# Summing Strassen-Winograd weight quarters with adding DMA transfers, and FFN 2 without plain tiles

## The chip, the cores and the metric

One core of one Trainium2 chip runs the whole block in one launch. The metric is the device time of the execution in microseconds (us). The kernel before takes 1122.21 us (median of three runs, 1121.78 to 1122.27). TensorE is the matrix engine (PE in the profile; PEld is its weight load), VectorE is DVE, ScalarE is ACT, GpSimd is POOL, and SyncE (SP) issues most transfers.

## The reference

One encoder layer on 512 tokens with 1024 features, in float32:

```python
x = x + 0.5 * swiglu(rmsnorm(x, norm_ffn1), w_ffn1_gu, w_ffn1_down)
h = rmsnorm(x, norm_mix) @ w_in      # 7 x 1024 columns
# RG-LRU branch (conv, two scans) and 2-D neighbourhood attention, gated and summed to y
x = x + y @ w_out
x = x + 0.5 * swiglu(rmsnorm(x, norm_ffn2), w_ffn2_gu, w_ffn2_down)

def swiglu(h, w_gu, w_down):         # D_FF = 2816
    g, u = split(h @ w_gu, 2)
    return (silu(g) * u) @ w_down
```

The change is in the product with `w_gu` of the two feed-forward networks, FFN 1 and FFN 2 (1024 x 5632 each).

## The kernel before, in words

Activations lie with features on the 128 partitions and tokens along the free axis, as eight tiles (k = 0 to 7) of 128 x 512. A float32 product is made of three matmuls: each operand is split into a rounded high part H and the rest L, and H·H, H·L and L·H are added up in PSUM. Activations are split once; each weight tile of 128 x 1024 is loaded by SP (512 KB), copied to H by ScalarE, and L = raw − H is made by VectorE (`split`, lines 136 to 141). There are three raw weight buffers (`wraw`), four H/L pairs (`wh`, `wl`), and four `pair` tiles of the same size as a raw one.

The hidden tiles of an FFN (22 tiles of 128) are made in two ways. The first `NPLAIN` (4 in FFN 1, 2 in FFN 2) are **plain**: a chunk of 24 matmuls of 512 columns for the gate half, another for the up half (`feat_chunk`, lines 165 to 167). The rest go two at a time, in **units**, by the seven products of the Strassen-Winograd scheme (`strassen`; FFN 1 has 9 units, FFN 2 has 10). A unit's weight block is cut into four quarters of 128 x 1024 (numbered 0 to 3 in the source tensor), the activations into quarters by features and tokens. A product is 24 matmuls of 256 columns (line 291). Seven weight operands are needed: the quarters 0, 2 and 3 themselves, and four sums. Tile `a_` starts as quarter 0 and grows in place: + quarter 1 (form s1), + quarter 3 (form s2), + quarter 2 (for the last product, a22). Tile `b_` is quarter 3 (form s4), then + quarter 1 (form s3). VectorE makes these four adds (line 325), from quarters that stay in their tiles. Each operand is split before the next add changes its tile.

TensorE's order in a unit is a11 (into Z), a12 (into Y), s1, the a22 product of the unit before, s2, s4, s3. In the last unit of an FFN a12 comes after s3, and then its own a22. Between them VectorE and ScalarE add up, multiply by the reciprocal root of the norm, and apply SiLU (`gate`, `put`).

`rstd` makes that reciprocal root: four transposes on TensorE (line 213, or four small matmuls in FFN 1), a reduction and a scaling on VectorE, a square root on ScalarE, a reciprocal on VectorE, four more transposes (line 221), and a copy. In FFN 2 it stands between the first two plain chunks. The activation forms s1 to s4 of FFN 2 (`make_forms`) are made while the last tiles of the product with `w_out` come in.

The order within an engine is not written out: the Tile scheduler takes the program's order as its priority, moves work marked `high_priority` ahead, and places the semaphores. The engines then run their queues in order.

Of the kernel before, what the change touches and what calls it, by code (L numbers as in the profile page):

```python
# [9 lines left out]
F32 = mybir.dt.float32  # L10
F32R = mybir.dt.float32r
AF = mybir.ActivationFunctionType
ALU = mybir.AluOpType
# [3 lines left out]
P = 128  # L17
T = 512
D = 1024
KT = D // P  # L20
DFF = 2816
FT = DFF // P
# [20 lines left out]
NLEAD = 6  # L43


NPLAIN = 4, 2

DTAIL = 3

# [2 lines left out]
AHEAD = 4  # L52
# [32 lines left out]
def block_kernel(ctx: ExitStack, tc, a, out):  # L85
    nc = tc.nc
    const = ctx.enter_context(tc.tile_pool(name="const", bufs=1))
    wpool = ctx.enter_context(tc.tile_pool(name="wpool", bufs=3))
    xpool = ctx.enter_context(tc.tile_pool(name="xpool", bufs=1))
# [11 lines left out]
    def nm(s):  # L101
        uid[0] += 1
        return f"{s}_{uid[0]}"
# [3 lines left out]
    def big_t(dt=F32, shape=(P, T), n="b"):  # L107
        return big.tile(list(shape), dt, tag="big", bufs=NBIG, name=nm(n))
# [13 lines left out]
    xd = dram.tile([KT, P, T], F32, name="xd")  # L122
# [22 lines left out]
    def raw_t():  # L145
        return wpool.tile([P, 1024], F32, tag="wraw", bufs=3, name=nm("wraw"))
# [53 lines left out]

        return xh, xl, ssum, one, square

    def rstd(ssum, lead=False):

        pc = aux_t()
        vx = tiny.tile([P, NCB], F32, tag="vx", name=nm("vx"))
        if lead:
            for j in range(NCB):
                nc.tensor.matmul(pc[:, j : j + 1], ssum[:, j * P : (j + 1) * P], ones[:, 0:1], start=True, stop=True)
            nc.vector.tensor_scalar(vx, pc[:, 0:NCB], 1.0 / D, EPS, ALU.mult, ALU.add)  # L210
        else:
            for j in range(NCB):
                nc.tensor.transpose(pc[:, j * P : (j + 1) * P], ssum[:, j * P : (j + 1) * P], ident)
            nc.vector.reduce_sum(vx, pc.rearrange("p (j f) -> p j f", j=NCB), axis=AX.X)
            nc.vector.tensor_scalar(vx, vx, 1.0 / D, EPS, ALU.mult, ALU.add)
        rcol = tiny.tile([P, NCB], F32, tag="rcol", name=nm("rcol"))
        nc.scalar.activation(rcol, vx, AF.Sqrt)
        nc.vector.reciprocal(rcol, rcol)
        ps = aux_t()
        for j in range(NCB):  # L220
            nc.tensor.transpose(ps[:, j * P : (j + 1) * P], rcol[:, j : j + 1].to_broadcast([P, P]), ident)
        r = xpool.tile([P, T], F32, tag="rstd", name=nm("rstd"))
        nc.scalar.activation(r, ps, AF.Copy)
        return r, rcol, vx

# [46 lines left out]

        return S, raw, cut

    def strassen(src, units, A, r, hs, ahead):

        half = T // 2
        prev = {}
        view = lambda t: t.rearrange("p (m t) -> p m t", m=2)

        def product(ps, w, form, first, last):
            H, L = w
            for m in range(2):
                o = ps[:, m * half : (m + 1) * half]
                for k in range(4):
                    c = slice((m * 4 + k) * P, (m * 4 + k + 1) * P)
                    xh_, xl_ = A[form][k]


                    for w_, x_ in ((H, xh_), (H, xl_), (L, xh_)):  # L290
                        nc.tensor.matmul(o, w_[:, c], x_, start=first and m + k == 0 and w_ is H and x_ is xh_,  # L291
                                         stop=m + k == 4 and w_ is L, skip_group_check=True)

        def operand(raw):
            w = hl_t()
            with tc.high_priority():
                split(raw, *w)
            return w

        def gate(t, tok):  # L300
            rr = r[:, tok].unsqueeze(1).to_broadcast([P, 2, half])
            s_ = big_t(n="s")
            nc.vector.tensor_tensor(view(s_), view(t), rr, ALU.mult)
            nc.scalar.activation(s_, s_, AF.Silu)
            return s_

        def put(u, s_, t, tok):
            for m in range(2):
                c = slice(m * half, (m + 1) * half)
                mark["h"] = nc.vector.tensor_tensor(hs[u * 2 + m][:, tok], s_[:, c], t[:, c], ALU.mult)  # L310

        def last_product(p):
            product(p["Z"], p["w"](), "a22", False, True)
            put(p["u"], gate(p["Z"], slice(half, T)), p["u7"], slice(half, T))

        for u in range(units):
            a_, b_ = raw_t(), raw_t()
            d = pair_t().rearrange("p a b -> p (a b)")
            c = pair_t().rearrange("p a b -> p (a b)")

            for t, i in ((a_, 0), (d, 1), (b_, 3), (c, 2)):
                nc.sync.dma_start(t, src[u, i])

            def add(t, o, i):
                nc.vector.tensor_tensor(t, t, o, ALU.add)  # L325
            def after_sum(t, o, i, add=add):
                with tc.high_priority():
                    add(t, o, i)
                return operand(t)

            Z, X, Y = acc_t(), acc_t(), aux_t()
            hs += [big_t(n="h") for _ in range(2)]
            last = u == units - 1

            def gate1():
                product(Y, w_c, "a12", True, True)
                nc.vector.tensor_tensor(p1, p1, Y, ALU.add)
                return gate(p1, slice(0, half))

            product(Z, operand(a_), "a11", True, False)  # L340
            p1 = big_t(n="p1")
            nc.scalar.activation(p1, Z, AF.Copy)
            w_c = operand(c)
            if not last:
                s1 = gate1()
            product(X, after_sum(a_, d, 1), "s1", True, False)
            p5 = big_t(n="p5")
            nc.scalar.activation(p5, X, AF.Copy)
            if prev:
                last_product(prev)  # L350
            product(Z, after_sum(a_, b_, 3), "s2", False, False)
            u2 = big_t(n="u2")
            nc.scalar.activation(u2, Z, AF.Copy)
            product(X, operand(b_), "s4", False, True)
            nc.vector.tensor_tensor(u2, u2, X, ALU.add)
            product(Z, after_sum(b_, d, 1), "s3", False, False)
            nc.vector.tensor_tensor(p5, p5, Z, ALU.add)
            if last:
                ahead()
                s1 = gate1()  # L360
            put(len(hs) // 2 - 1, s1, u2, slice(0, half))
            prev = dict(u=len(hs) // 2 - 1, Z=Z, u7=p5, w=lambda a_=a_, c=c, f=after_sum: f(a_, c, 2))
        last_product(prev)

    def ffn(wgu, ws, wd, xh, xl, S, ssum, plain, res, emit_out, lead=None, end=None):
        hs = []
        r = None
        pre = {}
        if lead is not None:
# [5 lines left out]
            for k in range(KT):  # L375
                lead[0](k)
                if k in LEAD_W:
                    n = LEAD_W[k]
                    o = (k % 4) * P
# [53 lines left out]
        A = {"a11": quarter(0, slice(0, half)), "a12": quarter(4, slice(0, half)),  # L433
             "a22": quarter(4, slice(half, T)), **S}
# [5 lines left out]
        def ahead(n):  # L440
            while len(cuts) < min(n, len(order)):
                qk = order[len(cuts)]
                cuts[qk] = big_t(F32R, n="hh"), big_t(F32R, n="hl")
                split(hs[qk[1]], *cuts[qk])

        strassen(ws, (FT - plain) // 2, A, r, hs, lambda: ahead(AHEAD))
        for q in range(2):
            outs = range(q * 4, q * 4 + 4)
            for i in range(2):
                t = pair_t()  # L450
# [23 lines left out]
            for i, m in enumerate(outs):  # L474
# [4 lines left out]
                t = big_t(n="dn")  # L479
# [50 lines left out]
    xh, xl, ssum, one, square = make_xg(C_G1, "a")  # L530
# [32 lines left out]
    forms = Forms(C_G1)  # L563
# [20 lines left out]
    xh, xl, ssum = nxt["v"][:3]  # L584
# [424 lines left out]
    def out2(m, ps):  # L1009
# [1 line left out]
        nc.vector.tensor_tensor(o, ps, xres[m], ALU.add)  # L1011
        nc.sync.dma_start(out[m], o)

    ffn(a["w2gu"], a["w2s"], a["w2d"], xh, xl, forms.S, ssum, NPLAIN[1], lambda m: xd[m], out2,
        end=lambda tok, o: nc.sync.dma_start(out[KT - 1][:, tok], o[:, tok]))


def layouts(inp):
# [3 lines left out]
    o = {}  # L1022
# [7 lines left out]
    for i in (1, 2):  # L1030
        w = f(f"w_ffn{i}_gu")[0]
        g, u = feat(w[:, :DFF]), feat(w[:, DFF:])
        n = NPLAIN[i - 1]
        o[f"w{i}gu"] = con(np.stack([g, u], 1)[:n]).reshape(2 * n, P, D)

        b = np.stack([g, u], 0)[:, n:].reshape(2, (FT - n) // 2, 2, P, 2, D // 2)
        o[f"w{i}s"] = con(b.transpose(1, 4, 0, 3, 2, 5)).reshape((FT - n) // 2, 4, P, D)
        d = f(f"w_ffn{i}_down")[0].reshape(FT // 2, 2, P, 2, T)
        o[f"w{i}d"] = con(d.transpose(3, 0, 2, 1, 4)).reshape(2, FT // 2, P, 2 * T)
# [50 lines left out]
```

## Time and profile before

| | |
|---|---|
| median of three runs | 1122.21 us |
| profiled execution | 1122.16 us |
| its span, first to last instruction | 1119.9 us |
| TensorE busy | 1113.1 us |
| VectorE busy | 835.1 us |
| ScalarE busy | 593.0 us |
| GpSimd busy | 52.4 us |
| mean DMA rate | 123 GB/s |
| TensorE clock granted | 1.00 |

FFN 1's units run from about 45 to 233 us of the span, the mixing part follows, the product with `w_out` ends at about 772, FFN 2's plain chunks at 795, its units at 997. A row of the page's groups gives line, engine, operation, output and inputs, shapes and count, then busy us and mean ns of one, then the idle time before. A row of the timeline or of the chain begins with start and duration in us. A row of the windows view gives the stretch, its length, then for PE, PEld, DVE, ACT and POOL the busy time and count, then the granted clock, the DMA engines' busy share and GB/s. A DMA row gives count, KB each and the median us from issue to landing.

### The profile page before, as it was taken

How to read it: one execution, taken by the hardware profiler on the slowest of the kernel's cores; microseconds unless marked ns; L12 is line 12 of the kernel's file. 1: busy time of each engine (PE TensorE's matmuls, PEld its weight loads, DVE VectorE, ACT ScalarE, POOL GpSimd, SP SyncE). 2: the span in 40 equal slices, each digit the busy share in tenths (PEclk: the TensorE clock that was granted, in tenths of full speed). 3: DMA queues.
4: the chain of work that ended last, by engine and by line, in shares of the span. 5: the costliest groups of instructions: out<-in, count | busy, mean ns of one | idle time of the engine just before them, and what ended most of it. 6: DMA issues, size and time to landing. Idle time of an engine off the chain costs nothing.

```text
span 1119.9 us, 17423 instructions
## 1 busy us (share of the span) xinstructions
PE 1113.1 (99%) x6867; PEld 983.9 (88%) x6867; DVE 835.1 (75%) x1294; ACT 593.0 (53%) x897; POOL 52.4 (5%) x116
## 2 busy tenths in 40 slices
PE   9999999999999999999999999999999999999998
PEld 8899999988888778787888888888999999998887
DVE  7888888894745776998655976659788888894552
ACT  8554554563533669876464564446445455464330
POOL 0000000000000341310110000000000000000000
PEclk9999999999999999999999999999999999999999
DMA  7232333343433585653443332264134233353421
GB/s 265 95 124 85 113 114 95 120 144 95 136 91 107 160 255 154 184 164 95 144 140 104 104 104 72 75 237 164 57 96 131 77 115 113 94 170 95 132 76 38
DMA packets 46770, 138.04 MB, mean 123 GB/s; under 512 B 7008, under 2 KB 10592, under 8 KB 46688
## 3 DMA queue, kind: packets, MB, share of 16 engines
q1 hardware_dynamic: 39744, 118.31, 33.9%
q0 software_dynamic: 6368, 18.36, 5.8%
q8 instruction: 54, 0.88, 0.3%
q10 hardware_dynamic: 576, 0.26, 0.1%
q14 instruction: 28, 0.23, 0.1%
HBM read 120.12 MB, written 8.39 MB: 115 GB/s over the span
## 4 chain that ended last, share of the span: by engine, by line
PE 99%; DVE 0%; ACT 0%; issue 0%; ACTq 0%; DVEq 0%
PE acc L291 29%; PE acc L165 11%; PE acc L166 11%; PE acc L167 11%; PE aux L291 5%; PE acc L763 4%; PE acc L765 4%; PE acc L764 4%; PE aux L165 4%; PE aux L166 4%; PE aux L167 4%; PE aux L898 1%; PE aux L886 1%; PE aux L677 1%; PE aux L857 1%; PE acc L404 1%
## 5 line engine op out<-in xcount | busy, mean ns | idle before, releaser
L138 ACT ACTIVATE wh<-wraw 128x1024 fp32r<-128x1024 f32 (+3 forms) x242 | 239.7, 993 | 304.3 <-PE acc L291 95.9
L141 DVE TENSOR_TENSOR wl<-wraw,wh 128x1024 fp32r<-128x1024 f32 (+3 forms) x254 | 289.1, 1143 | 135.7 <-ACT wh L138 134.7
L291 PE MATMUL acc<-s,wh 128*128 128x256 f32 x1216 | 220.5, 283 | 0.0
L291 PEld LDWEIGHTS acc<-s,wh 128*128 128x128 f32 x1216 | 189.7, 192 | 0.0
L291 PE MATMUL acc<-s,wl 128*128 128x256 f32 x608 | 172.1, 283 | 0.0
L165 PE MATMUL acc<-xh,wh 128*128 128x512 f32 x304 | 121.1, 399 | 0.0
L167 PE MATMUL acc<-xh,wl 128*128 128x512 f32 x304 | 119.0, 391 | 0.0
L166 PE MATMUL acc<-xl,wh 128*128 128x512 f32 x304 | 118.9, 391 | 0.0
L291 PEld LDWEIGHTS acc<-s,wl 128*128 128x128 f32 x608 | 116.7, 192 | 0.0
L291 PE MATMUL acc<-xh,wl 128*128 128x256 f32 x304 | 86.0, 283 | 0.0
L291 PE MATMUL acc<-xl,wh 128*128 128x256 f32 x304 | 86.0, 283 | 0.0
L291 PE MATMUL acc<-xh,wh 128*128 128x256 f32 x304 | 86.0, 283 | 0.0
L763 PE MATMUL acc<-wh,xh 128*128 128x512 f32 x192 | 75.6, 394 | 0.0
L765 PE MATMUL acc<-wl,xh 128*128 128x512 f32 x192 | 74.9, 390 | 0.0
L764 PE MATMUL acc<-wh,xl 128*128 128x512 f32 x192 | 74.9, 390 | 0.0
L325 DVE TENSOR_TENSOR wraw<-wraw,pair 128x1024 f32<-128x1024 f32 x57 | 69.6, 1220 | 0.8
L165 PE MATMUL aux<-hh,wh 128*128 128x512 f32 (+1 forms) x181 | 69.9, 386 | 0.0
L166 PE MATMUL aux<-hl,wh 128*128 128x512 f32 (+1 forms) x181 | 69.9, 386 | 0.0
L167 PE MATMUL aux<-hh,wl 128*128 128x512 f32 (+1 forms) x181 | 69.9, 386 | 0.0
L165 PEld LDWEIGHTS acc<-xh,wh 128*128 128x128 f32 x304 | 57.1, 188 | 12.8 <-issue 1.7
L167 PE MATMUL acc<-hh,wl 128*128 128x512 f32 (+1 forms) x176 | 67.9, 386 | 0.0
L166 PE MATMUL acc<-hl,wh 128*128 128x512 f32 (+1 forms) x176 | 67.9, 386 | 0.0
(212 smaller groups left out, 2215.6 us busy)
## 6 DMA issues: line engine op xcount, KB each, us to landing
wraw<-wqkv SPq DMA_DIRECT2D x24, 512.0 KB, 4.8
wraw<-wg SPq DMA_DIRECT2D x24, 512.0 KB, 3.6
wraw<-w1d SPq DMA_DIRECT2D x22, 512.0 KB, 3.6
wraw<-w2d SPq DMA_DIRECT2D x22, 512.0 KB, 3.6
pair<-w2s SPq DMA_DIRECT2D x20, 512.0 KB, 3.6
wraw<-w2s SPq DMA_DIRECT2D x20, 512.0 KB, 3.7
wraw<-w1s SPq DMA_DIRECT2D x18, 512.0 KB, 3.6
pair<-w1s SPq DMA_DIRECT2D x18, 512.0 KB, 3.6
```

The lines of the kernel that those rows point to most:

```text
L138: nc.scalar.activation(H, raw, AF.Copy)
L141: nc.vector.tensor_tensor(L, raw, H.bitcast(F32), ALU.subtract)
L165: nc.tensor.matmul(ps, wh, xh, start=first, stop=False, skip_group_check=skip)
L166: nc.tensor.matmul(ps, wh, xl, start=False, stop=False, skip_group_check=skip)
L167: mark["mm"] = nc.tensor.matmul(ps, wl, xh, start=False, stop=last, skip_group_check=skip)
L291: nc.tensor.matmul(o, w_[:, c], x_, start=first and m + k == 0 and w_ is H and x_ is xh_, stop=m + k == 4 and w_ is L, skip_group_check=True)
L325: nc.vector.tensor_tensor(t, t, o, ALU.add)
L404: nc.tensor.matmul(pre[i], w[i][1][:, s], xh[k], start=k == 0, stop=False)
L677: prev, mm = mm, nc.tensor.matmul(ps[d][b], W[w][o, c], X[x][o], start=x == 1, stop=w + x == 0)
L763: nc.tensor.matmul(pss[j], xh[kk][:, tj], H[:, s], start=kk == 0, stop=False)
L764: nc.tensor.matmul(pss[j], xl[kk][:, tj], H[:, s], start=False, stop=False)
L765: mark["mm"] = nc.tensor.matmul(pss[j], xh[kk][:, tj], L[:, s], start=False, stop=kk == KT - 1)
```

## The change

`NPLAIN` becomes 4, 0: FFN 2 has no plain tile and eleven units. In every unit of both FFNs the four adds leave VectorE. A transfer issued by GpSimd reads the quarter from memory and adds it into the tile (`accum_op=ALU.add`): quarters 1, 3 and 2 into `a_`, and quarter 3 into `d`, which was loaded as quarter 1 (form s3; before, it was made in `b_`). A unit so has four loads and four adding transfers of 512 KB each, where it had four loads. In FFN 2 the first products (a11) of units 0 and 1 are made first of all, by `begin`, and `rstd` is called after unit 0's a12, writing into a tile made beforehand.

```diff
-NPLAIN = 4, 2
+NPLAIN = 4, 0
...
+        def begin(u):
+            a_ = raw_t()
+            nc.sync.dma_start(a_, src[u, 0])
+            Z = acc_t()
             product(Z, operand(a_), "a11", True, False)
             p1 = big_t(n="p1")
             nc.scalar.activation(p1, Z, AF.Copy)
+            return a_, Z, p1
+
+        def add(u, t, i):
+            with tc.high_priority():
+                nc.gpsimd.dma_start(t, src[u, i], accum_op=ALU.add)
+
+        begun = {u: begin(u) for u in range(2)} if late is not None else {}
+        for u in range(units):
+            a_, Z, p1 = begun.pop(u) if u in begun else begin(u)
+            b_ = raw_t()
...
-            for t, i in ((a_, 0), (d, 1), (b_, 3), (c, 2)):
+            add(u, a_, 1)
+            for t, i in ((c, 2), (d, 1), (b_, 3)):
                 nc.sync.dma_start(t, src[u, i])
-            def add(t, o, i):
-                nc.vector.tensor_tensor(t, t, o, ALU.add)
+            add(u, d, 3)
...
                 product(Y, w_c, "a12", True, True)
+                if u == 0 and late is not None:
+                    late()
...
-            product(X, after_sum(a_, d, 1), "s1", True, False)
+            w = operand(a_)
+            add(u, a_, 3)
+            product(X, w, "s1", True, False)
...
-            product(Z, after_sum(a_, b_, 3), "s2", False, False)
+            w = operand(a_)
+            add(u, a_, 2)
+            product(Z, w, "s2", False, False)
...
-            product(Z, after_sum(b_, d, 1), "s3", False, False)
+            product(Z, operand(d), "s3", False, False)
...
-            prev = dict(..., w=lambda a_=a_, c=c, f=after_sum: f(a_, c, 2))
+            prev = dict(..., w=lambda a_=a_: operand(a_))
...
+        if r is None:
+            r = xpool.tile([P, T], F32, tag="rstd", name=nm("rstd"))
+            late = lambda: rstd(ssum, False, r)
```

GpSimd's queue of the new kernel, at the start of FFN 2 (`wraw_1429` and `wraw_1434` are the tiles a of units 0 and 1, `pair_1440`, `pair_1464` and `pair_1492` the tiles d of units 0, 1 and 2):

```order
L329 DMA pair_1440_7848<-w2s 128x1024
L329 DMA wraw_1429_7781<-w2s 128x1024
L329 DMA wraw_1434_7814<-w2s 128x1024
L329 DMA pair_1464_8031<-w2s 128x1024
L329 DMA wraw_1429_7781<-w2s 128x1024 x2
L329 DMA pair_1492_8263<-w2s 128x1024
L329 DMA wraw_1434_7814<-w2s 128x1024 x2
```

Before, GpSimd has nothing in this place. The add into the next unit's d now stands between a's first add and its second; the third follows the second.

VectorE's queue of the new kernel at the start of FFN 2, after the first two form splits (`wl_1457`, `wl_1460`, `wl_1462` are L of s2, s4 and s3 of unit 0, `wl_1471` is L of a12 of unit 1, `vx` and `rcol` belong to `rstd`):

```order
L141 TENSOR_TENSOR s2_1423_7769<-s2_1411_7713,s2_1422_7768 128x512
L141 TENSOR_TENSOR s4_1425_7773<-s4_1412_7715,s4_1424_7772 128x512
L141 TENSOR_TENSOR wl_1457_7940<-wraw_1429_7781,wh_1456_7939 128x1024
L141 TENSOR_TENSOR wl_1460_7971<-wraw_1439_7847,wh_1459_7970 128x1024
L141 TENSOR_TENSOR s3_1427_7777<-s3_1413_7717,s3_1426_7776 128x512
L141 TENSOR_TENSOR wl_1462_8000<-pair_1440_7848,wh_1461_7999 128x1024
L214 TENSOR_REDUCE vx_1449_7888<-aux_1448_7887 128x4
L350 TENSOR_TENSOR p1_1433_7812<-p1_1433_7812,aux_1443_7856 128x512
L215 TENSOR_SCALAR vx_1449_7888<-vx_1449_7888 128x4
L141 TENSOR_TENSOR wl_1471_8043<-pair_1465_8032,wh_1470_8042 128x1024
L218 RECIPROCAL rcol_1450_7895<-rcol_1450_7895 128x4
```

Before, the reduction (line 214) stood right behind the first of these rows, and the reciprocal five rows later. Now three weight splits and a form split stand ahead of the reduction, and one more split ahead of the reciprocal.

TensorE's queue of the new kernel at the second transposes of `rstd` (line 221), with the end of s2 of unit 0 ahead (`wh_1456`, `wl_1457`) and a12 of unit 1 behind (`wh_1470`):

```order
L292 MATMUL acc_1430_7783<-s2_1422_7768,wh_1456_7939 128x256
L292 MATMUL acc_1430_7783<-s2_1423_7769,wh_1456_7939 128x256
L221 MATMUL aux_1451_7898<-ident_83,rcol_1450_7895 128x128 x4
L292 MATMUL acc_1430_7783<-s2_1422_7768,wl_1457_7940 128x256
L292 MATMUL aux_1467_8039<-xh_1352_7421,wh_1470_8042 128x256
```

Before, these transposes stood in the second plain chunk. They now stand one matmul before the end of the fifth product of FFN 2.

More of the change, by code (lines that the diff above doesn't have):

```diff
@@ L201, in make_xg, with rstd @@
         return xh, xl, ssum, one, square
-    def rstd(ssum, lead=False):
+    def rstd(ssum, lead=False, r=None):
         pc = aux_t()
@@ L221, in rstd @@
             nc.tensor.transpose(ps[:, j * P : (j + 1) * P], rcol[:, j : j + 1].to_broadcast([P, P]), ident)
-        r = xpool.tile([P, T], F32, tag="rstd", name=nm("rstd"))
+        if r is None:
+            r = xpool.tile([P, T], F32, tag="rstd", name=nm("rstd"))
         nc.scalar.activation(r, ps, AF.Copy)
@@ L273, in make_forms, with strassen @@
         return S, raw, cut
-    def strassen(src, units, A, r, hs, ahead):
+    def strassen(src, units, A, r, hs, ahead, late=None):
         half = T // 2
@@ L314, in last_product @@
             put(p["u"], gate(p["Z"], slice(half, T)), p["u7"], slice(half, T))
+        def begin(u):
+            a_ = raw_t()
+            nc.sync.dma_start(a_, src[u, 0])
+            Z = acc_t()
+            product(Z, operand(a_), "a11", True, False)
+            p1 = big_t(n="p1")
+            nc.scalar.activation(p1, Z, AF.Copy)
+            return a_, Z, p1
[3 more added lines that the diff above has]
+        begun = {u: begin(u) for u in range(2)} if late is not None else {}
         for u in range(units):
-            a_, b_ = raw_t(), raw_t()
+            a_, Z, p1 = begun.pop(u) if u in begun else begin(u)
+            b_ = raw_t()
             d = pair_t().rearrange("p a b -> p (a b)")
             c = pair_t().rearrange("p a b -> p (a b)")
-            for t, i in ((a_, 0), (d, 1), (b_, 3), (c, 2)):
+            add(u, a_, 1)
+            for t, i in ((c, 2), (d, 1), (b_, 3)):
                 nc.sync.dma_start(t, src[u, i])
-            def add(t, o, i):
[L325 to L331, printed above, removed]
+            add(u, d, 3)
+            X, Y = acc_t(), aux_t()
             hs += [big_t(n="h") for _ in range(2)]
@@ L336, in gate1 @@
                 product(Y, w_c, "a12", True, True)
+                if u == 0 and late is not None:
+                    late()
                 nc.vector.tensor_tensor(p1, p1, Y, ALU.add)
                 return gate(p1, slice(0, half))
-            product(Z, operand(a_), "a11", True, False)
-            p1 = big_t(n="p1")
-            nc.scalar.activation(p1, Z, AF.Copy)
             w_c = operand(c)
@@ L361, in strassen @@
             put(len(hs) // 2 - 1, s1, u2, slice(0, half))
-            prev = dict(u=len(hs) // 2 - 1, Z=Z, u7=p5, w=lambda a_=a_, c=c, f=after_sum: f(a_, c, 2))
+            prev = dict(u=len(hs) // 2 - 1, Z=Z, u7=p5, w=lambda a_=a_: operand(a_))
         last_product(prev)
@@ L444, in ahead @@
                 split(hs[qk[1]], *cuts[qk])
-        strassen(ws, (FT - plain) // 2, A, r, hs, lambda: ahead(AHEAD))
+        if r is None:
+            r = xpool.tile([P, T], F32, tag="rstd", name=nm("rstd"))
+            late = lambda: rstd(ssum, False, r)
+        else:
+            late = None
+        strassen(ws, (FT - plain) // 2, A, r, hs, lambda: ahead(AHEAD), late)
         for q in range(2):
@@ L1012, in out2 @@
         nc.sync.dma_start(out[m], o)
-    ffn(a["w2gu"], a["w2s"], a["w2d"], xh, xl, forms.S, ssum, NPLAIN[1], lambda m: xd[m], out2,
+    ffn(None, a["w2s"], a["w2d"], xh, xl, forms.S, ssum, NPLAIN[1], lambda m: xd[m], out2,
         end=lambda tok, o: nc.sync.dma_start(out[KT - 1][:, tok], o[:, tok]))
@@ L1033, in layouts @@
         n = NPLAIN[i - 1]
-        o[f"w{i}gu"] = con(np.stack([g, u], 1)[:n]).reshape(2 * n, P, D)
+        if n:
+            o[f"w{i}gu"] = con(np.stack([g, u], 1)[:n]).reshape(2 * n, P, D)
         b = np.stack([g, u], 0)[:, n:].reshape(2, (FT - n) // 2, 2, P, 2, D // 2)
```

## The prediction

> **What bounds the kernel now.** I read the page first: engines, then the chain that ended last.
>
> ```profile
> span 1119.9 us, 17423 instructions
> ...
> PE 1113.1 (99%) x6867; PEld 983.9 (88%) x6867; DVE 835.1 (75%) x1294; ACT 593.0 (53%) x897; POOL 52.4 (5%) x116
> ...
> PE 99%; DVE 0%; ACT 0%; issue 0%; ACTq 0%; DVEq 0%
> ```
>
> TensorE is busy for 1113.1 of 1119.9 us, and the chain is TensorE all the way. Only two things can shorten the kernel: less TensorE work, or some of its 6.8 idle us. VectorE time as such buys nothing. Where TensorE stands in the two places that the change touches is read from the chain in order of time, FFN 1's start first, then FFN 2:
>
> ```profile
> 56.51 5.65 PE acc L291 x47
> ...
> 62.41 0.95 ACT wh L138
> ...
> 63.41 0.50 PE aux L291 x2
> ```
> ```profile
> 777.68 0.44 PE aux L213 x4
> ...
> 784.72 0.44 PE aux L221 x4
> ...
> 794.93 2.87 PE acc L291 x24
> ...
> 858.29 17.28 PE acc L291 x144
> 875.57 2.88 PE aux L291 x24
> 878.45 17.28 PE acc L291 x144
> 895.73 2.88 PE aux L291 x24
> ```
>
> FFN 1 has one hole, about 0.9 us at 62.4, where a weight operand was late. FFN 2's seven-product units run without one: a product of 24 matmuls takes 2.88 us, a unit 7 x 2.88 = 20.16 us. The windows view shows the four plain chunks and one unit:
>
> ```profile
> 772.24:794.93 22.69, 22.69 (x106) 18.79 (x106) 16.48 (x26) 12.81 (x18) 0.00 (x0) 1.00 0.18 63
> 878.45:898.61 20.16, 20.16 (x170) 20.16 (x170) 17.27 (x21) 10.15 (x13) 0.00 (x0) 1.00 0.34 105
> ```
>
> **The change, part by part. Plain chunks for a unit.** The first window holds the 96 plain matmuls and the 8 transposes of the reciprocal root (2 x 0.44 us): 22.69 - 0.88 = 21.8 us for 96. They go, the transposes stay, and an eleventh unit of 20.16 us comes: -1.6 us. That is the whole of the arithmetic gain, although an eighth of the multiplications is saved, because a 512-column matmul costs 0.227 us and a 256-column one 0.120.
>
> **Adds taken from VectorE.** The groups view has them on one line:
>
> ```profile
> L325 DVE TENSOR_TENSOR wraw<-wraw,pair 128x1024 f32<-128x1024 f32 x57 | 69.6, 1220 | 0.8
> ...
> L325 DVE TENSOR_TENSOR wraw<-wraw,wraw 128x1024 f32<-128x1024 f32 x19 | 23.2, 1220 | 0.1
> ```
>
> 92.8 us leave VectorE. All but FFN 1's hole lies under TensorE, so I credit -0.9 us: in the new order the first unit's fourth and fifth products follow its third, and no add stands before their splits. The transposes of FFN 1's own root move some matmuls earlier there; I put that at nothing, +-0.4 us, as vector work and matmuls stand close on both sides.
>
> **The price of an adding transfer, X** (issue to landing). No row shows one. The nearest rows:
>
> ```profile
> wraw<-w2s SPq DMA_DIRECT2D x20, 512.0 KB, 3.7
> ...
> bm<-rpb POOLq DMA_DIRECT2D x16, 384.0 KB, 4.7
> ...
> wraw<-wgate SPq DMA_DIRECT2D x8, 128.0 KB, 2.8
> ```
> ```profile
> L805 POOL DMA_DIRECT2D bm<-rpb x16: 548/548/608, 405.4 to 649.5; - x16
> ...
> DMA to landing us min/median/max: 3.2/4.7/8.3
> ```
>
> Lower bound: 3.7 us, a plain load of these bytes (the 3.2 us of GpSimd's quickest 384 KB say that its queue alone is no slower). Upper bound: 7.4 us, two such loads one behind the other. In between, 128 to 512 KB cost 0.9 us, so 512 KB of data cost 1.2 us and the rest is fixed; if the transfer must read the old sum as well as the quarter, 3.7 + 1.2 = 4.9. Some traffic beside it adds, up to the 8.3 - 4.7 of the row above at worst; I take X = 5.3 us.
>
> The Trainium skill (Collectives: The Full Stack, "The bandwidth ceiling") says that an adding transfer is slower because it needs two source reads, not because of the addition, with half the rate measured. No run here shows it yet. With the fit of DMA: Bandwidth & Descriptors ("Anatomy of one DMA"), 2.0 us plus bytes over 436 GB/s, that is an estimate of 2.0 + 2 x 1.2 = 4.4 us, and the sum below would be about 1.7 us lower by it.
>
> **What waits for X.** Each split is a ScalarE copy (H) and a VectorE subtraction (L). Of a unit's four adds three hit one tile, a: split, add, split, add, split, add, split. An in-place add may start only when L of the form before has been read out. The timeline of before gives the clock of such splits; they start when a product frees one of four operand buffers:
>
> ```profile
> 884.17 1.06 ACT L138 ACTIVATE wh<-wraw 128x1024 fp32r<-128x1024 f32 x1 [0.44 <-PE acc L291]
> ```
> ```profile
> 885.51 1.21 DVE L141 TENSOR_TENSOR wl<-wraw,wh 128x1024 fp32r<-128x1024 f32 x1
> ...
> 891.14 1.22 DVE L141 TENSOR_TENSOR wl<-wraw,wh 128x1024 fp32r<-128x1024 f32 x1
> ```
>
> For the unit whose a11 product starts at 892.85 (2.88 before 895.73), the first split of a ends at 886.72. The first add then lands at 886.8 + X; H 1.06, L 1.22 and two hand-overs make 2.35, so the second form is split at 889.15 + X, or at 892.36 as before, if that is later. The second add lands at 889.2 + 2X. Its form, s2, is the fifth product, at 892.85 + 4 x 2.88 = 904.37, and needs L by its third matmul, 904.6; less 2.35 that is 902.25. So 2X must stay under 13.05: **a middle unit is covered up to X = 6.5 us.** In GpSimd's queue the next unit's add into d stands behind the first add, but its load landed by then, so it is not waited for. The third add has five products of time.
>
> In each FFN's last unit the a12 product is put behind the others, so s2 comes 2.88 us sooner: covered up to 2X = 10.17, and short by 2X - 10.2 beyond. At 5.3: 0.4 us, twice, +0.8.
>
> **FFN 2's start.** The root now stands behind the first three products. Until 778.6 the order on ScalarE and VectorE is that of before, four plain splits replaced by a11, a11 of the second unit, c and s1, so its times hold:
>
> ```profile
> 773.55 1.22 DVE L141 TENSOR_TENSOR wl<-wraw,wh 128x1024 fp32r<-128x1024 f32 x1
> ...
> 778.62 0.68 DVE L214 TENSOR_REDUCE vx<-aux 128x4 f32<-128x512 f32 x1
> ...
> 782.09 0.68 DVE L141 TENSOR_TENSOR s<-s,s 128x512 fp32r<-128x512 f32 x1
> 782.69 0.16 DVE L215 TENSOR_SCALAR vx<-vx 128x4 f32<-128x4 f32 x1
> 783.12 0.18 DVE L218 RECIPROCAL rcol<-rcol 128x4 f32<-128x4 f32 x1 [0.27 <-ACT rcol L217]
> ```
>
> The fourth split (s1) ends at 774.8; then a's second add goes out, with d's add of the second unit just ahead in the same queue (+0.5), and lands at 774.8 + 5.3 + 0.5 = 780.6. VectorE now has, in order: L of s2, L of s4, the last form's split, L of s3, the reduction, p1 + Y, the scaling, L of the second unit's a12, the reciprocal. H of s2 first, 1.1; then 1.22 + 1.22 + 0.68 + 1.22 + 0.68 + 0.68 + 0.16 + 1.22 + 0.18 = 7.3, less 0.4, as back-to-back instructions overlap by some 0.08 us: the reciprocal is there at 780.6 + 8.0 = 788.6. TensorE reaches the second transposes, one matmul before the end of s2, at 772.24 + 3 x 2.88 + 0.44 + 2.88 + 23 x 0.12 = 786.96, and stands: **+1.6 us**. Behind it stand that matmul, the second unit's a12 and s4; they have their operands by then. s2 itself needs H by 784.2 and has it at 781.7. The stall is X + 0.5 - 4.2; below X = 3.7 it is nothing.
>
> **The sum**, against the profiled execution: 1122.16 us (span 1119.9 and 2.3 around it, 0.05 under the median 1122.21). -1.6 - 0.9 + 1.6 + 0.8 = -0.1, so **1122.1 us**. A measurement here tells 0.2% (2.2 us) from no change.
>
> **The rivals.**
>
> *Faster: the add is nearly free.* X near 3.7: no stall at the start, none in the last units, -2.5 us, 1119.7. For it: the 3.2 us row. Against it: a transfer that reads twice as much would have to take no longer. All gains lie in FFN 1's hole and the 1.6 us, so there is nothing below about 1119.5.
>
> *Slower, by the start and the last units.* X of 5.8 to 6.5, say 6.2: start 2.5, last units 2 x 2.2, so -2.5 + 6.9 = +4.4, 1126.6. For it: the 4.7 us median of GpSimd's loads, with 1.2 for the second read.
>
> *Slower, by the chain of adds in every unit.* One mechanism, split-add-split-add before s2, deciding from X = 6.5: a unit then takes X - 6.5 more (each stall before s2 also starts the next unit's chain that much sooner in its cycle, so 2(X - 6.5) shares out over two). At 7.3: 17 middle units x 0.8 = 13.6, last units 2 x 3.6, start 3.6, less 2.5: +22, 1144. For it: the chain hangs on a latency that nothing here has measured. Against it: the upper bound has to be nearly right.
>
> *Slower, by full DMA engines.* A unit's four loads take 0.34 of 20.16 us, 1.7 each. Four adds at twice that would make 6.9 + 13.7 = 20.6 us, more than a unit: 20 x 0.4, about +9, 1131. The Trainium skill (DMA: Bandwidth & Descriptors, "Issuing engines are not separate DMA queues") is on its side: all transfers share 16 engines, and GpSimd's queue saves only issue time. Against it a stage of before:
>
> ```profile
> 0.00:45.00 45.00, 43.94 (x196) 36.88 (x197) 35.83 (x78) 31.96 (x58) 0.83 (x10) 1.00 0.66 223
> ```
>
> 223 GB/s at a share of 0.66 is 338 at full; the unit would read 6.3 MB in 20.16 us, 312 GB/s. Tight, but under it.
>
> That the change might not do what it says I give nothing: the new order holds 80 adding transfers, and no plain chunk in FFN 2.
>
> **How the numbers follow.** No change 0.47 (X about 3.9 to 5.75, 1120 to 1124.4); faster 0.20; slower by start and ends 0.13; by the chain 0.16; by full engines 0.04. Faster by over 0.2%: 0.20, though its case ends close to that bound; within: 0.47; slower: 0.33. The range is 1119.4, with all holes closed, to 1129, X = 6.5 with start 2.8 and last units 2 x 2.8 (1128) and a little of the chain; most of the chain case is left out.
>
> **What would show it.** The adding transfers' landing time is X; below 3.9, or above 5.8, my case falls. A hole of 1 to 2 us before the second transposes of FFN 2, some 14 us after its first product; none at FFN 1's start; under a microsecond each before s2 of the two last units; units of 20.16 us between. A unit longer than 20.16 would prove the chain, if TensorE waits before s2 for ScalarE's split and that for a transfer; full engines, if the DMA share in the unit is over 0.95. A DMA share of about 0.9 in a unit would bear out the second read, and one near 0.68 would refute it.

## The result, and the profile after

The changed kernel takes **1194.76 us** (median of four, 1191.06 to 1196.26), against 1122.24 for the kernel before: a ratio of 1.0642, 95% interval 1.0629 to 1.0655. The forecast was 1122.1 us, no change, with a range up to 1129.0; the measured time is 72.7 us above it.

The page of the changed kernel: span, busy times, and the adding transfers, whose issue-to-landing time stands at the end of their row.

```profile
span 1193.3 us, 17696 instructions
...
PE 1138.8 (95%) x6939; PEld 1000.4 (84%) x6939; DVE 753.1 (63%) x1226; ACT 587.8 (49%) x903; POOL 120.9 (10%) x196
...
wraw<-w2s POOLq DMA_DIRECT2D x33, 512.0 KB, 5.7
```

VectorE is relieved by 82 us net (the adds alone were 92.8). TensorE now stands idle for 54.5 us where it was 6.8. It is also busy for 25.7 us longer, though its matmuls were to take 1.6 us less: behind some holes its granted clock is halved (the last experiment), and the mean of the matmuls with s and wh on line 292 is 294 ns where the same ones took 283. What it waits for is told by the waits view (engine, tile and line waited for, us in total, times, longest):

```profile
PE acc L292 <- DVE wl L141: 14.6, 20, 0.8
PE acc L292 <- ACT wh L138: 12.9, 15, 2.1
PE acc L292 <- ACT u L367: 10.1, 14, 5.2
PE acc L292 <- ACT p L360: 6.3, 12, 0.5
PE acc L292 <- ACT p L324: 4.6, 1, 4.6
```

Apart from the last row, and from the one of 5.2 us in the third, these are small holes, repeated from unit to unit. One step back, ScalarE's waits show where they come from:

```profile
ACT wh L138 <- DMA wraw<-w2s: 120.8, 21, 7.4
ACT wh L138 <- DMA wraw<-w1s: 106.3, 18, 8.8
```

Before, ScalarE's splits in the units waited for TensorE to free an operand buffer (107.6 us in 87 waits). Now they wait for the transfers into `wraw`, 227 us in 39 waits, about two a unit.

Half of the loss is in each FFN. A wait in the middle of the mixing part, whose order is the same in both kernels, gives the border; first before, then after:

```profile
517.31 0.39 PE L857 MATMUL aux<-kl,qh 64*128 64x256 f32 x2 [0.90 <-DVE kl L840]
```
```profile
551.94 0.39 PE L876 MATMUL aux<-kl,qh 64*128 64x256 f32 x2 [0.91 <-DVE kl L859]
```

So 34.6 us are lost in FFN 1 and 73.4 - 34.6 = 38.8 in FFN 2 with its new start.

**The rhythm of a unit.** ScalarE's timeline shows one unit of FFN 2 from its s1 split to that of the next; GpSimd's gives the adds.

```profile
903.25 2.01 ACT L138 ACTIVATE wh<-wraw 128x1024 fp32r<-128x1024 f32 x2 [6.61 <-DMA wraw<-w2s]
...
911.21 2.00 ACT L138 ACTIVATE wh<-wraw 128x1024 fp32r<-128x1024 f32 x2 [5.46 <-DMA wraw<-w2s]
914.88 0.63 ACT L305 ACTIVATE s<-s 128x512 f32<-128x512 f32 x1 [1.67 <-DVE s L304]
915.42 1.04 ACT L138 ACTIVATE wh<-pair 128x1024 fp32r<-128x1024 f32 x1
916.37 0.58 ACT L360 ACTIVATE p<-acc 128x512 f32<-128x512 f32 x1
916.84 1.05 ACT L138 ACTIVATE wh<-wraw 128x1024 fp32r<-128x1024 f32 x1
...
926.21 2.00 ACT L138 ACTIVATE wh<-wraw 128x1024 fp32r<-128x1024 f32 x2 [5.79 <-DMA wraw<-w2s]
```
```profile
905.93 0.85 POOL L329 DMA_DIRECT2D wraw<-w2s  x1 [6.21 <-DVE h L311]
913.88 0.87 POOL L329 DMA_DIRECT2D wraw<-w2s  x1 [7.10 <-DVE wl L141]
919.94 0.87 POOL L329 DMA_DIRECT2D wraw<-w2s  x1 [5.19 <-DVE wl L141]
```

Each pair "x2" is two splits: at 903.25 s1 and the a22 of the unit before, at 911.21 s2 and s4. The s1 split starts at 903.25 and is read out by 905.6. The second add goes out at 905.93 and has landed by 911.21, where s2 is split. Behind s2 on ScalarE stand s4, a SiLU, s3 (`pair`) and the copy of the s1 product; only at 916.84 comes the split of the **next unit's a11**. When VectorE has read that out, the next unit's first add may start, at 919.94; it lands, and the next s1 split starts at 926.21. (The add at 913.88 is the third, for a22.) This is a closed loop: 2.7 + 5.3 + 5.6 + 3.1 + 6.3 = 23.0 us, of which 5.3 and 6.3 are landings and 11.4 splits and queues. TensorE's 20.16 us of work are not in it.

From 72.19 to 235.73 there are seven such rounds in FFN 1, 23.36 us each; from 855.66 to 1041.97 eight in FFN 2, 23.29 each:

```profile
72.19 2.01 ACT L138 ACTIVATE wh<-wraw 128x1024 fp32r<-128x1024 f32 x2 [8.76 <-DMA wraw<-w1s]
...
235.73 2.01 ACT L138 ACTIVATE wh<-wraw 128x1024 fp32r<-128x1024 f32 x2 [5.20 <-DMA wraw<-w1s]
...
855.66 2.01 ACT L138 ACTIVATE wh<-wraw 128x1024 fp32r<-128x1024 f32 x2 [7.40 <-DMA wraw<-w2s]
...
1041.97 2.01 ACT L138 ACTIVATE wh<-wraw 128x1024 fp32r<-128x1024 f32 x2 [5.24 <-DMA wraw<-w2s]
```

These 15 rounds lose 7 x 3.20 + 8 x 3.13 = 47 us of the 73. The other 26 lie in the first and last units and are only in part itemised here, by two single holes: 4.62 us before FFN 2's fifth product, and 5.16 us in FFN 1's last unit, where s3 waits for ScalarE's copy of the s2 product, which stands behind the split of a22, and that behind the third add, which landed after 8.8 us.

```profile
823.40 0.80 PE L292 MATMUL acc<-s,wh 128*128 128x256 f32 x2 [4.62 <-ACT p L324]
```
```profile
257.14 0.80 PE L292 MATMUL acc<-s,wh 128*128 128x256 f32 x2 [5.16 <-ACT u L367]
```

### The profile page after: what moved, and what is told of

Same layout as the page of the kernel before. It is cut to its first block, busy times and chain, and to the rows that moved or that the text cites. A ratio compares the mean times of both kernels' runs of the same rounds, so it can differ in the third digit from the quotient of the medians.

```text
span 1193.3 us, 17696 instructions
## 1 busy us (share of the span) xinstructions
PE 1138.8 (95%) x6939; PEld 1000.4 (84%) x6939; DVE 753.1 (63%) x1226; ACT 587.8 (49%) x903; POOL 120.9 (10%) x196
## 5 line engine op out<-in xcount | busy, mean ns | idle before, releaser
L141 DVE TENSOR_TENSOR wl<-wraw,wh 128x1024 fp32r<-128x1024 f32 (+3 forms) x236 | 267.0, 1137 | 293.4 <-ACT wh L138 287.6
L138 ACT ACTIVATE wh<-wraw 128x1024 fp32r<-128x1024 f32 (+3 forms) x224 | 216.4, 983 | 398.5 <-DMA wraw<-w2s 120.8
L292 PE MATMUL acc<-s,wh 128*128 128x256 f32 x1280 | 248.8, 294 | 34.0 <-ACT wh L138 12.9
L292 PEld LDWEIGHTS acc<-s,wh 128*128 128x128 f32 x1280 | 207.7, 200 | 43.0 <-ACT wh L138 16.3
L292 PE MATMUL acc<-s,wl 128*128 128x256 f32 x640 | 188.4, 294 | 14.6 <-DVE wl L141 14.6
L292 PEld LDWEIGHTS acc<-s,wl 128*128 128x128 f32 x640 | 127.7, 200 | 18.9 <-DVE wl L141 18.7
L165 PE MATMUL acc<-xh,wh 128*128 128x512 f32 x272 | 108.6, 399 | 0.0
L167 PE MATMUL acc<-xh,wl 128*128 128x512 f32 x272 | 106.4, 391 | 0.0
L166 PE MATMUL acc<-xl,wh 128*128 128x512 f32 x272 | 106.3, 391 | 0.0
L165 PE MATMUL acc<-hh,wh 128*128 128x512 f32 (+1 forms) x176 | 67.9, 386 | 0.0
```

Source lines behind the costliest of these rows:

```text
L138: nc.scalar.activation(H, raw, AF.Copy)
L141: nc.vector.tensor_tensor(L, raw, H.bitcast(F32), ALU.subtract)
L165: nc.tensor.matmul(ps, wh, xh, start=first, stop=False, skip_group_check=skip)
L166: nc.tensor.matmul(ps, wh, xl, start=False, stop=False, skip_group_check=skip)
L167: mark["mm"] = nc.tensor.matmul(ps, wl, xh, start=False, stop=last, skip_group_check=skip)
```

## The experiments

**Theories.** A: the loop just read off sets a unit's time. B: the transfer engines are too full (busy 0.78 in the units), so that bytes set it. C: FFN 2's new start is what costs. D, tried last: TensorE's halved clock after the holes.

**The price of one adding transfer.** Edit, behind the last output of the kernel before:

```diff
+    t = raw_t()
+    for kind in ("sync", "pool", "add"):
+        for n in (1024, 512, 256):
+            for j in range(3):
+                q = nc.sync if kind == "sync" else nc.gpsimd
+                kw = dict(accum_op=ALU.add) if kind == "add" else {}
+                i = q.dma_start(t[:, :n], w[j, 0][:, :n], **kw)
+                after(i, prev, True)
+                prev = i
```

> The kernel before, with 27 transfers put behind its last output, each waiting for the one ahead: plain loads issued by SyncE, plain loads issued by GpSimd, adding transfers issued by GpSimd, three each of 512, 256 and 128 KB, into one idle tile. Nothing else moves then. Theory A (the adding transfer is dear by itself): 512 KB by adding takes at least 5.0 us from issue to landing, against 3.7 for a plain load, and falls by over 1 us at 256 KB. Theory B (it is dear in the units because the transfer engines are crowded there): under 4.5 us alone, and the 5.7 us of the changed kernel is mostly queueing. The time of this kernel is that of before plus the probes and says nothing.

The landing times (least, median, most of three), for 512 KB loaded plainly by GpSimd, and then for 512, 256 and 128 KB by adding, each from its own stretch:

```profile
DMA to landing us min/median/max: 3.8/3.9/4.0
```
```profile
DMA to landing us min/median/max: 5.7/5.7/5.8
```
```profile
DMA to landing us min/median/max: 3.5/3.8/3.8
```
```profile
DMA to landing us min/median/max: 3.0/3.0/3.1
```

With nothing beside it an adding transfer of 512 KB takes **5.7 us**, as the median in the units does. That price is its own, not queueing; B's reason for the 5.7 falls. Single landings in the changed kernel go from 5.2 to 12.7 us, so neighbours do add to it at times.

**The adds without the new start.** FFN 2 keeps two plain tiles; the rest is as changed.

```diff
-NPLAIN = 4, 0
+NPLAIN = 4, 2
```

> The adding transfers alone: FFN 2 keeps its two plain tiles, its root between them, and 10 units. Theory A (a closed loop of two adds and the splits between them, 23 us a round, in every unit of both FFNs): FFN 1 as in the changed kernel, +34 us, and FFN 2's 10 units +2.7 us each with its last unit, so 1180 to 1190 us. Theory C (the loss of FFN 2 comes from its new start, two first products and the late root): 1122 + 34 = 1156 to 1162 us.

Measured 1191.15 us in a single run, 3.6 less than the changed kernel's median and inside the spread of its four runs. Nearly all of the loss is there without the new start, whose own price cannot be read from this run; C falls as the main cause, and A's 1180 to 1190 was just missed.

**The new start without the adding transfers.**

```diff
-            add(u, a_, 1)
-            add(u, d, 3)
...
-            w = operand(a_)
-            add(u, a_, 3)
-            product(X, w, "s1", True, False)
+            product(X, after_sum(a_, d), "s1", True, False)
...
```

(with the three other sums in the same way by VectorE)

> The eleven units and the late root alone: FFN 2 without plain tiles, its first two products ahead, the four sums of every unit made by VectorE as before. Theory A: no loop over transfers, units of 20.16 us; four plain chunks for a unit, -1.6 us, and at most 1 us lost at FFN 2's start, so 1120 to 1122 us. Theory C (the new start loses): 1125 us or more, with a hole ahead of the fifth product or of the root's second transposes.

Measured 1126.09 us, ratio 1.0038 (1.0025 to 1.0050): 0.4% slower than before, where A had 1120 to 1122. One hole explains most of it:

```profile
786.08 0.39 PE L292 MATMUL acc<-s,wh 128*128 128x256 f32 x1 [4.23 <-DVE s L141]
```

The s1 product waits for the last split of its activation form; C had put the hole later, ahead of the fifth product or the second transposes. Four sums by VectorE now stand between the parts of the forms, where before four plain chunks gave 21.8 us of cover. Behind the hole the granted clock is 0.85 and 0.72 (784 to 788, 788 to 792), an estimated 1.7 us. So C is real in this kernel, at some 4 us and what the clock adds; and the two halves of the change need each other, since with the adds on transfers this hole is not there.

**The next unit's first product sooner.**

```diff
             nc.scalar.activation(u2, Z, AF.Copy)
+            if u + 1 < units and u + 1 not in begun:
+                begun[u + 1] = begin(u + 1)
```

> The changed kernel with one edit: the first product of the next unit is made right behind s2 of this one, two products sooner, so that its split stands ahead of those of s4 and s3 on ScalarE and VectorE, and the next add into its tile does not wait for them. The transfers and their bytes are the same. Theory A (closed loop, 2 landings + 11.4 us of splits and queues between): the 11.4 fall to about 7.5, the loop to 19 us, under the 20.16 us of TensorE, so middle units go back to 20.2 to 20.8 us and the whole to 1125 to 1145 us (FFN 2's start and the two last units keep their holes). Theory B (the transfer engines are full): the same 23 us a unit, 1185 to 1195 us.

Measured 1210.44 us, ratio 1.0782: slower still, a miss for A as it was put, and above B's range too. GpSimd's timeline and ScalarE's show why:

```profile
885.36 0.85 POOL L329 DMA_DIRECT2D pair<-w2s  x1 [8.04 <-DVE wl L141]
885.92 1.17 POOL L329 DMA_DIRECT2D wraw<-w2s  x1
...
900.85 0.84 POOL L329 DMA_DIRECT2D wraw<-w2s  x1 [1.62 <-DVE wl L141]
```
```profile
882.53 1.06 ACT L138 ACTIVATE wh<-wraw 128x1024 fp32r<-128x1024 f32 x1 [1.99 <-DMA wraw<-w2s]
...
895.72 2.01 ACT L138 ACTIVATE wh<-wraw 128x1024 fp32r<-128x1024 f32 x2 [10.08 <-DMA wraw<-w2s]
...
906.95 1.06 ACT L138 ACTIVATE wh<-wraw 128x1024 fp32r<-128x1024 f32 x1 [2.02 <-DMA wraw<-w2s]
```

The s1 split starts at 882.53, the second add goes out at 885.92, and at 895.72 s2 is split and, right behind it, the next unit's a11. The next first add goes out at 900.85, the next s1 split starts at 906.95. So the splits and queues did shrink, from 11.4 to 3.4 + 5.1 = 8.5 us. But the add into the next unit's d now goes out 0.6 us ahead of the loop's second add, and that one lands after 9.8 us instead of 5.3; with 6.1 us for the first add the round is 24.4 us. The loop stands; its landings are not a constant. From this run alone B could have been right, so the next pair keeps the bytes equal and takes that neighbour away.

**Three adds, in both orders.** The sum of s3 goes back to VectorE; once in the changed order, once with the product sooner.

```diff
-            add(u, d, 3)
...
-            product(Z, operand(d), "s3", False, False)
+            with tc.high_priority():
+                nc.vector.tensor_tensor(b_, b_, d, ALU.add)
+            product(Z, operand(b_), "s3", False, False)
```

> The changed kernel with the sum of s3 given back to VectorE (quarter 1 added into tile b after s4's split, as before): three adding transfers a unit where there were four, the order as changed. Theory A (a round of the loop is two landings of 5.7 us and the splits between them, 11.4 us; the add and the split of s3 stand on it, behind those of s4, and make it some 12.5): 23 to 24 us a unit, 1185 to 1205 us, though a quarter of the adding bytes is gone. Theory B (the transfer engines' throughput: they are 0.8 busy with four adds): a unit falls with the bytes, by 1.5 us or more, to under 1165 us.

> The kernel of the run before, with the first product of the next unit right behind s2, as tried above. The transfers and their bytes are those of the run before; only the order differs. The add into d, which stood right ahead of s2's add there and made that land after 9.8 us, is gone. Theory A: 6.1 + 5.7 us of landings and 8.5 us of splits make 20.3 us a round, so units of 20.2 to 20.8 us and 1125 to 1145 us, 50 us or more under the run before. Theory B: no difference between the two.

Each is a single run. In the changed order 1213.24 us, 8 us above A's range: a quarter of the adding bytes is gone, and it is slower, because s3's sum and split now stand on the loop (25.1 us a round in FFN 1). With the product sooner, and the same transfers, **1148.76 us**, 64 us less. This settles A against B. The size was a little off: the rounds take 21.4 us in FFN 2, not 20.2 to 20.8, and the total is 4 us over the range given. In two of these rounds the second add landed after 7.1 and 7.4 us, where 5.7 was put.

**One landing out of the loop.** The sum of s2 goes back to VectorE, three adding transfers as in the pair above, the order as changed.

```diff
-            add(u, a_, 3)
...
+            with tc.high_priority():
+                nc.vector.tensor_tensor(a_, a_, b_, ALU.add)
             w = operand(a_)
             add(u, a_, 2)
             product(Z, w, "s2", False, False)
```

> The changed kernel with the sum of s2 given back to VectorE (tile b added into tile a), the order as changed, three adding transfers a unit as in s3's case. Theory A: one landing of 5.7 us leaves the loop, one vector add of 1.2 us enters it, 18.5 us a round, less than TensorE's 20.16: units of 20.16 us, and 1120 to 1130 us, what is left being the start of FFN 2 and the last units. Theory B: the same as with s3's sum given back, since as many bytes move.

Measured 1123.21 us (ratio 1.0012, 1.0002 to 1.0021): as many adding bytes as the 1213 us kernel, 90 us less. In the units TensorE runs through; three holes are left, 1.62, 1.56 and 0.22 us.

**Plain loads in the adds' place.** The sums are left out here; all else stands.

```diff
-                nc.gpsimd.dma_start(t, src[u, i], accum_op=ALU.add)
+                nc.gpsimd.dma_start(t, src[u, i])
```

> The changed kernel with plain loads in the place of the adding transfers, same queue, same waits, same order; the sums are left out. Alone such a load lands after 3.9 us, an adding one after 5.7. Theory A: 2 x 3.9 + 11.4 = 19.2 us a round, under 20.16, so units of 20.16 to 20.5 us and 1122 to 1135 us. A rival (it is the waits between GpSimd and VectorE, not the time of the transfer): 1170 us or more.

Measured 1126.69 us; the loads into a land after 4.0 us:

```profile
wraw<-w2s POOLq DMA_DIRECT2D x33, 512.0 KB, 4.0
```

The same waits in the same order cost little (4.7 us, in a single run, with 2.5 of them ahead of FFN 2's fifth product) once 2 x 4.0 + 11.4 = 19.4 us is under TensorE's 20.16. So it is the transfers' duration, twice in the loop, and not the way over GpSimd. The DMA engines are less busy here too (0.65 in FFN 2's units), so against B the kernels with equal transfers above count, not this one.

**Closing what is left.** From the kernel with s2's sum on VectorE: first the last unit of each FFN wholly by VectorE; then also ScalarE's copy of the first product ahead of s2's split.

```diff
-            nc.scalar.activation(p1, Z, AF.Copy)
+            with tc.high_priority():
+                nc.scalar.activation(p1, Z, AF.Copy)
...
+            last = u == units - 1
+            if not last:
+                add(u, a_, 1)
...
+            if last:
+                with tc.high_priority():
+                    nc.vector.tensor_tensor(a_, a_, d, ALU.add)
...
```

(with the last unit's other sums in the same way; this edit also raises the priority of ScalarE's copy of the first product)

> The kernel with s2's sum on VectorE, and in the last unit of each FFN all four sums on VectorE. That kernel had three holes of its own: 1.6 us in FFN 1's last unit, 0.2 us in FFN 2's, 1.6 us ahead of FFN 2's fifth product, where TensorE waits for ScalarE's copy of the first product, which stands behind the split of the second unit's a12. Theory A: the first two close, so 1.8 us under that kernel's 1123.2: 1121.4 us (1120.5 to 1122). A rival (the last unit's sums on VectorE stand in front of the splits of the next product's operands): 1123 us or more.

```diff
+            if u == 0 and late is not None:
+                after(mark["H"], copies[0])
```

(`copies[0]` is the copy of the first product, `mark["H"]` the split put behind it; the raised priority is taken back)

> The kernel of the run before, with that copy put ahead of s2's weight split on ScalarE, behind the form splits. Theory A: the 1.6 us ahead of the fifth product go, or all but 0.5 us, since s2's split now stands behind the form splits: 1119.8 to 1120.8 us, the least that this order of products allows being about 1119.5. A rival (the form splits, now ahead of the weight splits, make s2's own operand late): a hole of 1 us or more in the same place, and no gain on the run before.

Measured 1120.88 (ratio 0.9989, 0.9981 to 0.9998) and **1119.76 us** (ratio 0.9980, 0.9971 to 0.9989): the second beats both kernels, the one before by 0.2%. The raised priority had left the hole ahead of FFN 2's fifth product as it was (1.57 us after 1.56); the explicit order removes it. All waits of its TensorE, and the stretch that is one unit before (columns as in the windows view above):

```profile
PE aux L131 <- DVE pol L637: 1.1, 1, 1.1
PE aux L892 <- DVE kl L875: 0.9, 1, 0.9
PE aux L221 <- DVE rcol L218: 0.7, 1, 0.7
PE aux L921 <- DVE nmx L904: 0.4, 1, 0.4
```
```profile
878.45:898.61 20.16, 20.16 (x170) 20.16 (x169) 13.88 (x18) 9.72 (x12) 2.50 (x3) 1.00 0.79 180
```

The DMA engines are as busy, 0.79, as in the slow kernel, with three adds in 20.16 us instead of four in 23.3, and no hole is left in the units.

**TensorE's clock.** After the holes the granted clock is halved for some microseconds in the changed kernel, in several places; here behind FFN 2's start:

```profile
824.00:828.00 4.00, 4.00 (x20) 4.00 (x20) 3.07 (x6) 2.27 (x3) 0.00 (x0) 0.50 1.02 238
```

Its mean is 0.987. Edit: six small matmuls of no use before s2 in each unit.

```diff
+            dummy = aux_t()
+            for _ in range(6):
+                nc.tensor.matmul(dummy[:, :P], ones, ones, start=True, stop=True)
             product(Z, w, "s2", False, False)
```

> The changed kernel with six small matmuls of no use (128 columns of ones, into an idle bank) ahead of s2's product in every unit, where TensorE stands anyway. They keep it busy through part of the hole. Theory D (the halved clock after the holes, 0.987 granted on the mean, is a part of the loss): the clock stays near 1.00 in the units and the kernel takes 5 to 12 us less than the changed one, 1183 to 1190 us. Theory A alone (the units are timed by the loop of adds and splits, and TensorE catches up whatever its clock): within 3 us of 1194.8, or a little above it.

The units of FFN 2, changed kernel first, then with the filler:

```profile
830.00:1052.00 222.00, 203.98 (x1603) 197.87 (x1601) 119.90 (x152) 91.76 (x116) 31.59 (x37) 0.98 0.76 177
```
```profile
830.00:1052.00 222.00, 213.14 (x1744) 208.93 (x1742) 120.02 (x151) 91.94 (x115) 31.49 (x37) 1.00 0.77 180
```

The clock stays at 1.00 there and the kernel takes 1197.31 us, none the less. A single run with work added does not price the clock, but D's 5 to 12 us are not there. That fits A: where the loop sets the time, a faster TensorE only waits longer. What the clock costs in the first and last units stays open.

## Why the prediction was wrong

**The step that failed: "a middle unit is covered up to X = 6.5 us".** I let the first split of a end at 886.72, as in the kernel before, and gave s2's split until 902.25, the latest that TensorE allows. Both cannot hold in the next unit, and the timeline of before said so. ScalarE's splits of one unit there, from s2 over s4 and s3 to the next a11:

```profile
895.69 1.06 ACT L138 ACTIVATE wh<-wraw 128x1024 fp32r<-128x1024 f32 x1 [1.81 <-PE acc L291]
898.57 1.06 ACT L138 ACTIVATE wh<-wraw 128x1024 fp32r<-128x1024 f32 x1 [1.33 <-issue]
902.83 1.06 ACT L138 ACTIVATE wh<-wraw 128x1024 fp32r<-128x1024 f32 x1 [0.19 <-DVE wraw L325]
904.33 1.06 ACT L138 ACTIVATE wh<-wraw 128x1024 fp32r<-128x1024 f32 x1 [0.44 <-PE acc L291]
```

The next a11 (904.33) stands behind s2 (895.69) in the same queue, and in this order could not follow it by less than the 5.6 us that s4, s3 and two small steps take in the changed kernel. Moved to 902.25, s2 would push it to 907.9 and with it the next unit's first add. I followed the chain to TensorE's deadline and stopped, where it ran on into the next unit. With the loop, the bound is 2X + 11.4 = 20.16, so X = 4.4 us, under my own X of 5.3: that X alone makes 2 x 5.3 + 11.4 = 22.0 us a unit, 1.8 too many, some 31 us over 17 middle units. My third rival named the right chain, with this wrong point; its sign came true too (a unit over 20.16 us, TensorE waiting before s2 for ScalarE's split and that for a transfer). In its sum the last units should be 2 x 4.4, since 2 x 7.3 - 10.2 is 4.4 and not 3.6: 1145.7 us, not 1144.

**X, mis-sized, but not the cause.** Taken 5.3, measured 5.7. By my sum 5.7 gives start 2.0 and last units 2 x 1.2, some 1124 us. The Trainium skill (Collectives: The Full Stack, "The bandwidth ceiling") gives a collective's ReduceScatter half the rate of its AllGather, because the add needs two source reads. The trace agrees with the factor: in the stretch of FFN 1 (60 to 260 us) the view shows GpSimd's adds (q0) beside SyncE's loads (q1), packets, MB and share of the engines:

```profile
q0 software_dynamic: 4513, 16.39, 49.2%
q1 hardware_dynamic: 5527, 18.05, 24.9%
```

That is 3.00 against 1.38 points per MB, 2.2 times; no run here shows that the second read is the reason. My own sign was a DMA share of about 0.9 in a unit of 20.16 us: the share of 0.77 over eight rounds of 23.29 us (855.66 to 1041.97) is 17.9 us of work a unit, 0.89 of 20.16, so that sign came, as far as a share can tell. The estimate of 4.4 us was too low all the same.

**FFN 2's start: near the right place, a landing mis-sized, and a wait left out.** Predicted +1.6 us at the second transposes, at the end of the fifth product, behind VectorE. The hole is 4.62 us, ahead of the fifth product. I let a's second add take X + 0.5 = 5.8 us behind the s1 split. GpSimd issued it 0.54 us behind the add into the second unit's d, and it took 9.3 (the issues of 809.46 and 810.00):

```profile
pair<-w2s POOLq DMA_DIRECT2D x1, 512.0 KB, 5.4
wraw<-w2s POOLq DMA_DIRECT2D x1, 512.0 KB, 9.3
```

And ScalarE had put its copies of the two first products behind the splits that wait for this add; s2 writes into the bank that the copy must have read.

```profile
819.40 2.00 ACT L138 ACTIVATE wh<-wraw 128x1024 fp32r<-128x1024 f32 x2 [5.96 <-DMA wraw<-w2s]
...
821.83 1.04 ACT L138 ACTIVATE wh<-pair 128x1024 fp32r<-128x1024 f32 x1
822.77 1.06 ACT L324 ACTIVATE p<-acc 128x512 f32<-128x512 f32 x2
```

I had laid out VectorE's queue there and left out ScalarE's. With s2's sum on VectorE, so without this landing, the hole is 1.56 us; with the copy also put ahead it is gone. From these two kernels I estimate some 3 us of it for the landing and the rest for the copy.

**Last units:** 0.4 us each predicted, ahead of s2; 5.16 us in FFN 1's, ahead of s3, by a copy that I had not placed. **What held:** the arithmetic, since the best variant's TensorE is busy for 1111.4 us, 1.7 less than before (-1.6 predicted); FFN 1's hole at 62.4, which is gone there and in the changed kernel; and 1119.5 as the least to be had, as far as these variants go (1119.76). **Full engines**, given 0.04, were not it: 0.79 busy in a kernel without holes.

## What to carry to other kernels

When work moves from an engine to a transfer, look for a cycle before looking at covers: follow each wait until it comes back to itself one iteration later, count every instruction queued in program order on the way, and compare the round with the bottleneck's time per iteration. A latency that is in the round twice costs twice in every iteration, however idle the engines are. A transfer issued right behind another can take much longer than one by itself, so put the neighbours in the count. Of several such moves, keep as many as the round has room for (here three adds of four), and leave the one that overfills it where it is quick.

## What the runs showed of the hardware

- A transfer that adds 512 KB in place takes 5.7 us alone, a plain one from the same queue 3.9, one from SyncE 3.6. From 256 to 512 KB adding costs 1.9 us more; at 128 KB it is 3.0 us.
- Two adding transfers issued 0.5 to 0.6 us apart by GpSimd: the second landed after 9.8 us with the first product sooner, and after 9.3 us at FFN 2's start of the changed kernel, against 5.3 in the round shown of the changed order.
- TensorE's clock was halved not only behind the 4.6 us hole: also behind one of 2.09 us, which ended at 865.89. It was 1.00 from 860 to 864 and 0.50 from 866 to 868, and stayed there behind a second hole of 0.46 us:

```profile
868.00:872.00 4.00, 4.00 (x20) 4.00 (x20) 3.49 (x5) 3.08 (x5) 0.31 (x1) 0.50 0.78 121
```

The Trainium skill (TensorE: Matmul & The Clock Gate, "Why this matters for your kernels") asks for no idle gap over about 3 us; here less sufficed.
